# Output projection of a hybrid encoder layer: five pairs of row chunks as seven block products, from chunk 6 on

## The chip, the core and the metric

The kernel runs on one core of a Trainium2 chip: TensorE (PE, matmuls, with its weight loads as PEld), VectorE (DVE), ScalarE (ACT), GpSimd (POOL) and SyncE (SP), which issues the DMAs, almost all of them on one queue. The metric is the time of one execution in microseconds (us) on the device; what counts is the median of several runs. Profiles are of one execution each; their times are microseconds from the start of the span unless marked ns.

## What is computed

One layer of an encoder over 2048 rows of 1024 values. An input projection feeds two groups: gated linear attention (4 heads, columns 0 to 511 of the mixer's output) and latent attention (4 heads, columns 512 to 1023). What matters here is the end of it:

```python
def mla_branch(...):
    ...
    o = o.transpose(1, 0, 2, 3, 4).reshape(B, S, D_MLA)
    return o * jax.nn.silu(gate)

def hybrid_mixer(...):
    ...
    return jnp.concatenate([o_a, o_b], axis=-1) @ w_out

def reference(...):
    ...
        x = layer_norm(DEEPNORM_ALPHA * x + mixed, ln_g[layer], ln_b[layer])
```

`o_a` is the first group's output, `o_b` the second's; the output projection is a product of 2048x1024 by 1024x1024, followed by the residual and the layer norm of each row.

## The kernel before

All matmuls work on float32 numbers split in two parts, hi (rounded) and lo (the rest): a product is three matmuls, hi by hi, hi by lo and lo by hi (`mm3`, L454 to L456). hi is made by ScalarE (L400), lo by GpSimd or VectorE (L406).

The rows are 16 chunks of 128. Attention (from L1615) sweeps 16 blocks, each of one head and 512 query rows; in the last block's steps the output projection begins. Chunks 0 to 3 are multiplied between the last block's matmuls. Then come chunks 4 to 7 one by one, and then chunks 8 to 15 in four pairs.

A **single chunk** (`OutProj`) is 2 halves of 512 columns times 8 slices of the contraction times 3 matmuls, 48 matmuls of 512 columns. Its steps are: `load` (four DMAs: `of` from `oa_s` and `ob_s`, the gates `gr` from `gm_s` and the reciprocal sums from `r_s`), `hi` and `lo` of the first group, `gate` (GpSimd, two products), `hi` and `lo` of the second, the matmuls (`part`), `residual` (VectorE: alpha times x plus the product, read from PSUM, and the statistics of the half row), `finish_a` (mean, centring, and on ScalarE six small operations for the reciprocal root, here called the roots) and `finish_b` (scale and shift on VectorE, two stores of 256 KB).

A **pair** (`Pair`) multiplies two chunks, seen as a 2x2 block matrix (rows of the two chunks, columns of the two groups), by the 2x2 block weight in Strassen's manner: seven products P1 to P7 of 4x3 matmuls, 84 in place of 96. S1 to S4 are sums of the blocks (VectorE), A11, A12, A22 the blocks themselves. Products 5, 6, 7 and 4 take combined weights, which are prepared early, kept in DRAM and fetched by `fetch_t` ("1h" to "4l"; "4h" and "4l" are four DMAs each and overwrite half of the plain weights, so they wait for the last single chunk). Four PSUM banks, `pw0` to `pw3` (tags mb, x, o, ap), hold the products: P1 and P7 go to bank 0, P5 and P2 to bank 1, P6 to 2, P3 and P4 to 3. `copy` (L2065) copies P1 and later P7 from bank 0 on ScalarE; `sum` adds the copy to bank 2; `read` adds the banks to the rows of x.

**What sets the order.** From chunk 6 on every step has a place, a number on a time axis in us at which it would stand on TensorE; `put` collects them, they are sorted by place, and `in_order` ties the instructions of each engine, SyncE with its DMAs included, to that order. A place orders, it makes nothing wait by itself. Pair p begins at 4 x 5.44 + 19.05 p, and `PLACE_PAIR` holds the places of its steps relative to that. In the stretch before (chunks 2 to 5) `fixed` ties only ScalarE, GpSimd and SyncE to the order of the program; VectorE and TensorE are ordered by the planner that builds the program.

**Buffers.** Tiles of one tag share slots; the first write into a slot waits until all that read or write the tile before have ended, stores by DMA included. Those that matter here:

- tag "ofl" (one slot): `ol` (lo part of the last block's output), then `yc`, then the copies `pc` of the pairs;
- tag "ph" (three slots): the result rows `rr` of single chunks, and the x rows of each pair's second chunk;
- tag "xf" (two slots): `of` of the single chunks from 4 on and of the even-numbered pairs; odd-numbered pairs use the two SBUF rows of the layer norm's parameters, after `ln_psum` has copied these to PSUM;
- `gr[0]`, `gr[1]`: the gates of even and odd chunks.

The last attention block is closed late: `tot`, `oh`, `ol` (its output, split), `tsum` and `rcp` (sums and their reciprocals), `turn` and `y` (a transpose and the product with the value weights), and `rows` and `yc`, which copy the results on ScalarE and store them by DMA (L1801 and L1824). Before the change these last four have the places 5.40 (`turn`), 5.41 (`y`), 6.50 (`rows`) and 6.51 (`yc`), with chunk 6 beginning at 0.

Of the kernel before, what the change touches and what calls it, by code (L numbers as in the profile page):

```python
# [9 lines left out]
F32 = mybir.dt.float32  # L10
# [8 lines left out]
P = 128  # L19
# [3 lines left out]
NCH = S // P  # L23
# [68 lines left out]
    tot=11.2,  # L92
    half=11.7,
    fold=11.95,
    tsum=12.37,
    rcp=13.55,
    keep=14.21,
    turn=17.5,
    rows=17.55,
    oh=12.34,  # L100
    ol=12.99,
    y=16.55,
    yc=16.9,
# [27 lines left out]
)  # L131


PAIR0, PAIR_US = 8, 19.05
PLACE_PAIR = dict(
    load3=(-29.4, -31.5),
    load2=(-25.5, -31.5),
# [7 lines left out]
    last=dict(P1=0.0, P5=2.72, P6=5.44, P3=8.16, P2=10.88, P7=13.6, P4=16.32),  # L145
# [244 lines left out]
class K:  # L390
# [1224 lines left out]
    def attention(self):  # L1615
# [4 lines left out]
        with ExitStack() as ctx:  # L1620
# [6 lines left out]
            nb = len(blocks)  # L1627
# [140 lines left out]
            def tsum(i):  # L1768
                d = stt[i]
                d["x"] = close(i, [P, 4, P], f"sx{i}", (pA, "ap"))  # L1770
                for e in range(4 if i == nb - 1 else 2):
                    nc.tensor.transpose(d["x"][:, e], d["as"][:, 0, e * P:(e + 1) * P], self.ident)
# [68 lines left out]
            def put(place, fn, *a):  # L1841
                todo.append((place, len(todo), fn, a))
# [7 lines left out]
            for i in range(nb):  # L1850
                for j in range(NP):
                    t = NP * i + j
# [52 lines left out]
            rest = {c: o for c, o in enumerate(first)}  # L1905

            def load(c):
                if c < NCH:
                    rest[c] = dict(c=c)
                    op.load(rest[c])  # L1910

            def split(c):
                if c < NCH:
                    op.hi(rest[c], 0)
                    op.lo(rest[c], 0)
                    if c == PAIR0 - 1:
                        op.ln_psum(1)
                    op.gate(rest[c])
                    op.hi(rest[c], 1)
                    op.lo(rest[c], 1)  # L1920

            pairs = [Pair(op, p, PAIR0 + 2 * p + 1, PAIR0 + 2 * p) for p in range((NCH - PAIR0) // 2)]
            with fixed():
                load(4)
                for c in (2, 3):
                    op.load_res(rest[c])
                load(5)
                split(4)
                load(6)
                op.load_res(rest[4])  # L1930
                for c in (0, 1):
                    op.finish(rest[c])
                split(5)
                load(7)
                op.load_res(rest[5])
                op.fetch_t("2l")
                op.fetch_t("3h")
                for c in (2, 3):
                    op.residual(rest[c], 0)
                    op.residual(rest[c], 1)  # L1940
                    op.finish(rest[c])
            for c in (4, 5):
                with fixed():
                    if c == 4:
                        split(6)
                        pairs[0].load(1)
                        op.product(rest[4])
                    else:
                        op.load_res(rest[6])
                        tsum(nb - 1)  # L1950
                        with self.after(rest[4]["last"]):
                            rcp(nb - 1)
                        op.product(rest[5])
                        op.ln_psum(0)
                        pairs[1].load(0, "of")
                        op.fetch_t("3m")
                        split(7)
                        pairs[0].load(0)
                    op.finish(rest[c])
                if c == 4:  # L1960
                    with self.after(*last.values()), fixed():
                        for f in (tot, oh, ol):
                            f(nb - 1)

            todo.clear()
            half = 5.44
            put(4 * half - 0.01, op.pair_banks)
            for c in (6, 7):
                o, t = rest[c], 2 * half * (c - 6)
                if c == 7:  # L1970
                    put(-1, op.load_res, o)
                for n in range(2):
                    for k in range(NK):
                        put(t + half * n, op.part, o, k, (n,))
                    put(t + half * (2 if c % 2 else n + 1) + 0.05, op.residual, o, n)
                put(t + 2 * half + 1.3, op.finish_a, o)
                put(t + 2 * half + (5 if c == 6 else 4), op.finish_b, o)
            for place, f in ((5.4, turn), (5.41, y), (6.5, rows), (6.51, yc)):
                put(place, f, nb - 1)
            put(17.15, op.fetch_t, "4h")  # L1980
            put(17.16, op.fetch_t, "4l")
            op.last_pair = pairs[-1]
# [7 lines left out]
class Pair:  # L1990
# [131 lines left out]
    def put(self, put, T, last):  # L2122
        at = lambda place, fn, *a: put(T + place, fn, *a)
        P_, op = PLACE_PAIR, self.op
        first = P_[("first", "second")[self.p]] if self.p < 2 else {}
        if self.p:
            for r in (1, 0):
                at(P_[f"load{self.p}"][r], self.load, r, *(("gr",),) * (self.p == 1 and r == 0))
        for r in range(2):
            at(P_["res"][r], self.load_res, r)  # L2130
            for n in range(2):
                at(P_[f"gate{self.p}" if self.p < 3 else "gate"][r][n], self.gate, r, n)
        for n in self.OPERANDS:
            if n[0] == "S":
                at(first.get(f"a{n}", P_["add"][n]), self.add, n)
            at(first.get(f"h{n}", P_["hi"][n]), self.hi, n)
            at(first.get(f"l{n}", P_["lo"][n]), self.lo, n)
        bank = [lambda i=i: op.pw[i] for i in range(4)]
        t = P_["last" if last else "product"]
        b = dict(P1=0, P5=1, P6=2, P3=3, P7=1 if last else 0, P2=0 if last else 1, P4=3)  # L2140
        for n in t:
            if not (last and n == "P4"):
                at(t[n], self.product, n, bank[b[n]])
        e = P_["read_last" if last else "read"]
        at(e["c1"], self.copy, bank[0])
        at(e["U2"], self.sum, bank[2])
        if last:
            reads = (("R1", 0, 0, 0), ("R5", 1, 1, 1), ("R5b", 0, 1, 1), ("R2", 0, 1, 2), ("R3", 1, 1, 2), ("R4b", 1, 0, 2),
                     ("R6", 0, 1, 3), ("R7", 0, 0, b["P2"]), ("R3p", 1, 1, b["P7"]), ("R4p", 1, 0, b["P7"]))
        else:  # L2150
            at(e["c7"], self.copy, bank[b["P7"]])
            at(e["U3"], self.sum, bank[2])
            reads = (("R1", 0, 0, 0), ("R5", 1, 1, 1), ("R5b", 0, 1, 1), ("R2", 0, 1, 2), ("R6", 0, 1, 3), ("R3", 1, 1, 2),
                     ("R7", 0, 0, b["P2"]), ("R4", 1, 0, 3), ("R4b", 1, 0, 2))
        for n, r, h, x in reads:
            at(e[n], self.read, r, h, bank[x])
        if not last:
            at(e["bn22"], self.stats, 1, 1, 1)
            at(e["bn21"], self.stats, 1, 0, 0)
            at(e["sq"], self.squares, 0)  # L2160
            at(e["rs"], self.scale, 0)
            at(e["fa"][0], self.centre, 0)
            at(e["fa"][1], op.finish_a, self.rows[1])
            for r in range(2):
                if op.last_pair.p == self.p + 1:
                    at(e["late"][r], op.last_pair.finish_off, self.rows[r])
                else:
                    at(e["fb"][r], op.finish_b, self.rows[r])
            return
        at(P_["lnb"], self.copy_lnb)  # L2170
        at(e["bn12"], self.stats, 0, 1, 1)
        at(e["bn11"], self.stats, 0, 0, 0)
        at(e["bn22"], self.stats, 1, 1, 2, 3)
        for i, x in enumerate((3, 0)):
            cs, half = slice(256 * i, 256 * i + 256), lambda x=x: bank[x]()[:, :256]
            at(t["P4"] + PAIR_US / 14 * i, self.product, "P4", half, cs)
            at(t["P4"] + PAIR_US / 14 * (i + 1) + 0.45, self.read, 1, 0, half, cs)
            at(t["P4"] + PAIR_US / 14 * (i + 1) + 0.46, self.stats, 1, 0, i, 3, cs)
        at(e["fa"][0], op.finish_a, self.rows[0])
        at(e["fb"][0], self.finish_off, self.rows[0])  # L2180
        at(e["fa"][1], op.finish_a, self.rows[1])
        at(e["fb"][1], op.finish_b, self.rows[1])


class OutProj:
# [110 lines left out]
    def banks(self, o):  # L2296

        c = o["c"]
        if c == PAIR0 - 1:
            return [p.tile([P, 512], F32, tag=t, name=f"p{t}{c}") for p, t in self.single[2:]]  # L2300
        if c < 2 or c % 2:
            ps = self.ps.tile([P, 2, 512], F32, tag="pS", name=f"po{c}")
            return [ps[:, 0], ps[:, 1]]
        return [p.tile([P, 512], F32, tag=t, name=f"p{t}{c}") for p, t in self.single[:2]]
# [128 lines left out]
```

## Time and profile before

| | |
|---|---|
| median of 3 runs | 1276.6 us (1276.45 to 1277.14) |
| the profiled execution | 1275.83 us, its span 1274.0 us |
| mean granted TensorE clock | 0.998 of full |
| TensorE busy | 1253.9 us, 98% of the span |
| VectorE, ScalarE, GpSimd busy | 74%, 69%, 67% |
| first matmul of chunk 4, of chunk 6, of the first pair | 1145.14, 1167.36, 1189.95 |

A row of a timeline reads: start, duration, engine, line, operation, what it writes <- what it reads, size, count, and in brackets the idle time ahead of it with what ended it. "SPq" is SyncE issuing a DMA; its duration is that of the issue (waits included where rows are merged), not of the transfer. `pw` is any of the four banks of the pairs, told apart by the operands: `pw<-woh,A11h` is P1, `pw<-wt3h,S3h` is P7. A window's row gives, for a stretch, the busy time of the engines, the granted clock, the busy share of the 16 DMA engines and what they moved.

### The profile page before, as it was taken

The page shows a single profiled execution, that of the slowest core. Times are in us where ns is not written, and L with a number is a line of the kernel's source. Part 1 is how long each engine was busy: PE and PEld are TensorE (multiplying, and loading weights), DVE is VectorE, ACT ScalarE, POOL GpSimd, SP SyncE. Part 2 cuts the span into 40 slices and gives each one's busy share as a digit, 9 for nine tenths or more (in the row PEclk, how much of TensorE's full clock was granted, in tenths as well). Part 3 has the DMA queues.
Part 4 walks back from the last instruction along what each step waited for, and adds up shares of the span by engine and source line. Part 5 has one row for each costly group of instructions (what it writes and reads, how often), then busy time and mean ns, then how long its engine had stood idle before and what let it go on. Part 6 is the DMA issues. An engine that isn't in the chain of part 4 may idle for free.

```text
span 1274.0 us, 20184 instructions
## 1 busy us (share of the span) xinstructions
PE 1253.9 (98%) x6928; PEld 1109.6 (87%) x6928; DVE 938.3 (74%) x1702; ACT 875.2 (69%) x1553; POOL 849.4 (67%) x550
## 2 busy tenths in 40 slices
PE   7999999999999999999999999999999999999997
PEld 7999999999989999999788888888888888788886
DVE  6866675656675455555798888888888888738897
ACT  7765656766675655665688888888888888624365
POOL 0144545363667666672188888889999999965774
PEclk9999999999999999999999999999999999999999
DMA  9332524353575565565601111121223111568962
GB/s 300 96 96 63 168 81 156 106 155 102 191 254 169 180 222 184 182 196 166 177 1 42 42 42 42 42 58 59 59 58 91 53 43 31 174 207 297 342 214 98
DMA packets 122518, 166.81 MB, mean 131 GB/s; under 512 B 18502, under 2 KB 71118, under 8 KB 121776
## 3 DMA queue, kind: packets, MB, share of 16 engines
q1 hardware_dynamic: 114256, 163.39, 40.2%
q0 software_dynamic: 768, 2.10, 0.5%
q8 instruction: 55, 0.90, 0.4%
q10 hardware_dynamic: 7392, 0.03, 0.3%
q14 instruction: 47, 0.39, 0.2%
HBM read 106.72 MB, written 58.75 MB: 130 GB/s over the span
## 4 chain that ended last, share of the span: by engine, by line
PE 88%; ACT 3%; POOL 2%; DVE 2%; DMA 2%; issue 1%; SPq 1%; DVEq 0%; POOLq 0%; ACTq 0%
PE o L454 4%; PE o L456 4%; PE pS L1649 4%; PE o L455 4%; PE pS L1651 4%; PE pS L1650 4%; PE pS L1652 4%; PE pS L1653 4%; PE ipa L454 4%; PE ipa L456 4%; PE ipa L455 4%; PE pz L455 2%; PE pz L456 2%; PE pz L454 2%; PE ipg L454 2%; PE ipg L455 2%
## 5 line engine op out<-in xcount | busy, mean ns | idle before, releaser
L406 POOL TENSOR_TENSOR pl<-s,ph 128x1024 fp32r<-128x1024 f32 x128 | 306.1, 2414 | 56.4 <-ACT ph L400 56.4
L1671 DVE TENSOR_TENSOR rm<-pS,rm 128x512 f32<-128x512 f32 x210 | 144.7, 689 | 26.3 <-ACT s L1658 20.7
L1695 DVE TENSOR_TENSOR s<-s,mb 128x1024 f32<-128x1024 f32 x128 | 151.1, 1212 | 9.4 <-PE mb L1689 9.3
L1658 ACT ACTIVATE s<-pS 128x1024 f32<-128x1024 f32 x128 | 131.2, 1025 | 37.6 <-PE pS L1653 33.2
L400 ACT ACTIVATE ph<-s 128x1024 fp32r<-128x1024 f32 x128 | 134.9, 1057 | 13.4 <-PE o L456 12.7
L1699 ACT ACTIVATE s<-s 128x1024 f32<-128x1024 f32 x128 | 131.4, 1051 | 13.4 <-DVE s L1695 13.3
L454 PE MATMUL ipa<-wah,xah 128*128 128x384 f32 (+1 forms) x384 | 130.2, 339 | 6.3 <-ACT wah L400 6.2
L1112 POOL TENSOR_TENSOR Us<-Us,cw 128x512 f32<-128x512 f32 x16 | 18.2, 1134 | 175.8 <-DVE Us L1110 167.7
L455 PE MATMUL ipa<-wal,xah 128*128 128x384 f32 (+1 forms) x384 | 125.2, 326 | 0.1
L456 PE MATMUL ipa<-wah,xal 128*128 128x384 f32 (+1 forms) x384 | 125.2, 326 | 0.0
L1649 PE MATMUL pS<-qh,ckvT_h 128*128 128x512 f32 x256 | 102.5, 401 | 0.8 <-DVE rm L1671 0.4
L454 PE MATMUL o<-ph,vh 128*128 128x512 f32 x256 | 101.1, 395 | 0.0
L1652 PE MATMUL pS<-rh,krs 128*128 128x512 f32 x256 | 99.8, 390 | 0.0
L1650 PE MATMUL pS<-ql,ckvT_h 128*128 128x512 f32 x256 | 99.8, 390 | 0.0
L456 PE MATMUL o<-ph,vl 128*128 128x512 f32 x256 | 99.8, 390 | 0.0
L1651 PE MATMUL pS<-qh,ckvT_l 128*128 128x512 f32 x256 | 99.8, 390 | 0.0
L1653 PE MATMUL pS<-rl,krs 128*128 128x512 f32 x256 | 99.8, 390 | 0.0
L455 PE MATMUL o<-pl,vh 128*128 128x512 f32 x256 | 99.8, 390 | 0.0
L1722 DVE TENSOR_TENSOR ap<-ap,s 128x512 f32<-128x512 f32 x120 | 83.1, 693 | 3.5 <-ACT ap L1714 0.7
L454 PEld LDWEIGHTS ipa<-wah,xah 128*128 128x128 f32 x384 | 73.4, 191 | 7.3 <-ACT wah L400 6.7
L454 PE MATMUL pz<-xch,wzh 128*128 128x256 f32 x256 | 74.8, 292 | 0.0
L455 PEld LDWEIGHTS ipa<-wal,xah 128*128 128x128 f32 x384 | 73.4, 191 | 1.3 <-DVE wal L406 0.7
(446 smaller groups left out, 3895.9 us busy)
## 6 DMA issues: line engine op xcount, KB each, us to landing
xcf<-xT_dram SPq DMA_DIRECT2D x16, 512.0 KB, 4.9
xr<-x_dram SPq DMA_DIRECT2D x16, 512.0 KB, 6.9
xaf<-xT_dram SPq DMA_DIRECT2D x14, 512.0 KB, 3.8
wb<-wO_dram SPq DMA_DIRECT2D x16, 256.0 KB, 3.0
oib<-oi_s SPq DMA_DIRECT2D x16, 256.0 KB, 3.8
qdb<-qd_s SPq DMA_DIRECT2D x16, 256.0 KB, 4.3
SU<-su_s SPq DMA_DIRECT2D x16, 256.0 KB, 4.6
ub<-u_s SPq DMA_DIRECT2D x16, 256.0 KB, 4.2
```

Of the source, the lines that this page charges most:

```text
L400: return nc.scalar.activation(dst, src, AF.Copy).ins
L406: return e.tensor_tensor(dst, src, hi.bitcast(F32), ALU.subtract).ins
L454: mm(out, ah, bh, start=start, stop=False)
L455: mm(out, ah, bl, start=False, stop=False)
L456: mm(out, al, bh, start=False, stop=stop)
L1649: mm(ps[:, e], kh, qh, start=True, stop=False)
L1650: mm(ps[:, e], kh, ql, start=False, stop=False)
L1651: mm(ps[:, e], kl, qh, start=False, stop=False)
L1652: mm(ps[:, e], kr, rh, start=False, stop=False)
L1653: mm(ps[:, e], kr, rl, start=False, stop=True)
L1671: V.tensor_tensor(d["rm"], src[:, e], d["rm"], ALU.max)
L1695: V.tensor_tensor(s, s, d["mb"][:, None, :].to_broadcast([P, 2, QB]), ALU.subtract)
```

## The change

The pairs begin with chunk 6 in place of chunk 8 (`PAIR0` 6), so that chunks 6 to 15 are five pairs, the first of chunks 7 and 6; only chunks 4 and 5 are multiplied singly, and they are now the ones ordered by place, with their first matmul at place 0. Of the pairs from the fourth on, the loads use the places `load3`.

In the fixed stretch `split` is cut in two halves (hi, lo and gate; second hi and lo). The `finish` of chunk 0 stands ahead of chunk 4's first half, that of chunk 1 between its halves, and that of chunk 2 between the halves of chunk 5; with them move their stores, on SyncE ahead of the loads that follow. `tot`, `oh` and `ol` of the last block come between chunk 4 and chunk 5. The loads of chunks 6 and 7 are those of the first pair.

In the part ordered by place, with chunk 4 at 0 and chunk 5 at 10.88: `ln_psum(0)` at 1.5, the second half of the second pair's loads at 6.4, `tsum` 10.87, `rcp` 10.90, `fetch_t("3m")` 11.9, `fetch_t("4h")` and `("4l")` at 17.15 and 17.16 as before, `turn` 21.70, `y` 21.71, `rows` 22.00, `yc` 22.01. Chunk 5 takes the banks mb and x, as chunk 4 does, and no longer the PSUM tiles "pS".

```diff
-PAIR0, PAIR_US = 8, 19.05
+PAIR0, PAIR_US = 6, 19.05
...
-            def split(c):
-                if c < NCH:
+            def split(c, j):
+                if j == 0:
                     op.hi(rest[c], 0)
                     op.lo(rest[c], 0)
                     if c == PAIR0 - 1:
                         op.ln_psum(1)
                     op.gate(rest[c])
+                else:
                     op.hi(rest[c], 1)
                     op.lo(rest[c], 1)
...
                 load(5)
-                split(4)
-                load(6)
+                op.finish(rest[0])
+                split(4, 0)
+                op.finish(rest[1])
+                split(4, 1)
+                op.residual(rest[2], 0)
+                op.residual(rest[2], 1)
+                pairs[0].load(1)
                 op.load_res(rest[4])
-                for c in (0, 1):
-                    op.finish(rest[c])
-                split(5)
-                load(7)
+                with self.after(*last.values()):
+                    for f in (tot, oh, ol):
+                        f(nb - 1)
+                split(5, 0)
+                op.finish(rest[2])
+                split(5, 1)
+                pairs[0].load(0)
                 op.load_res(rest[5])
                 op.fetch_t("2l")
                 op.fetch_t("3h")
-                for c in (2, 3):
-                    op.residual(rest[c], 0)
-                    op.residual(rest[c], 1)
-                    op.finish(rest[c])
-            for c in (4, 5):
...
+                op.residual(rest[3], 0)
+                op.residual(rest[3], 1)
+                op.finish(rest[3])
...
-            for c in (6, 7):
-                o, t = rest[c], 2 * half * (c - 6)
-                if c == 7:
-                    put(-1, op.load_res, o)
+            for c in (4, 5):
+                o, t = rest[c], 2 * half * (c - 4)
...
-                    put(t + half * (2 if c % 2 else n + 1) + 0.05, op.residual, o, n)
+                    put(t + half * (n + 1) + 0.05, op.residual, o, n)
...
-            for place, f in ((5.4, turn), (5.41, y), (6.5, rows), (6.51, yc)):
+            for place, f in ((10.87, tsum), (10.9, rcp), (21.7, turn), (21.71, y), (22.0, rows), (22.01, yc)):
                 put(place, f, nb - 1)
+            put(1.5, op.ln_psum, 0)
+            put(6.4, pairs[1].load, 0, "of")
+            put(11.9, op.fetch_t, "3m")
             put(17.15, op.fetch_t, "4h")
             put(17.16, op.fetch_t, "4l")
...
-                at(P_[f"load{self.p}"][r], self.load, r, *(("gr",),) * (self.p == 1 and r == 0))
+                at(P_[f"load{min(self.p, 3)}"][r], self.load, r, *(("gr",),) * (self.p == 1 and r == 0))
...
-        if c == PAIR0 - 1:
-            return [p.tile([P, 512], F32, tag=t, name=f"p{t}{c}") for p, t in self.single[2:]]
-        if c < 2 or c % 2:
+        if c < 2 or c == PAIR0 - 3:
```

More of the change, by code (lines that the diff above doesn't have):

```diff
@@ L1907, in load @@
             def load(c):
-                if c < NCH:
-                    rest[c] = dict(c=c)
-                    op.load(rest[c])
-            def split(c):
-                if c < NCH:
+                rest[c] = dict(c=c)
+                op.load(rest[c])
+            def split(c, j):
+                if j == 0:
                     op.hi(rest[c], 0)
@@ L1937, in attention @@
                 op.fetch_t("3h")
-                for c in (2, 3):
-                    op.residual(rest[c], 0)
-                    op.residual(rest[c], 1)
-                    op.finish(rest[c])
-            for c in (4, 5):
[L1943 to L1963, printed above, removed]
+                op.residual(rest[3], 0)
+                op.residual(rest[3], 1)
+                op.finish(rest[3])
             todo.clear()
@@ L1974, in attention @@
                         put(t + half * n, op.part, o, k, (n,))
[L1975 removed]
+                    put(t + half * (n + 1) + 0.05, op.residual, o, n)
                 put(t + 2 * half + 1.3, op.finish_a, o)
[L1977 to L1978 removed]
+                put(t + 2 * half + (5 if c == 4 else 4), op.finish_b, o)
+            for place, f in ((10.87, tsum), (10.9, rcp), (21.7, turn), (21.71, y), (22.0, rows), (22.01, yc)):
                 put(place, f, nb - 1)
+            put(1.5, op.ln_psum, 0)
+            put(6.4, pairs[1].load, 0, "of")
+            put(11.9, op.fetch_t, "3m")
             put(17.15, op.fetch_t, "4h")
```

## The prediction

> **What bounds the kernel now.** I read the page first (busy shares, then the chain that ended last), then TensorE's timeline from the end of attention on, then the same stretch of ScalarE and of SyncE's DMA queue, and last the windows.
>
> ```profile
> span 1274.0 us, 20184 instructions
> PE 1253.9 (98%) x6928; PEld 1109.6 (87%) x6928; DVE 938.3 (74%) x1702; ACT 875.2 (69%) x1553; POOL 849.4 (67%) x550
> ...
> PE 88%; ACT 3%; POOL 2%; DVE 2%; DMA 2%; issue 1%; SPq 1%; DVEq 0%; POOLq 0%; ACTq 0%
> ```
>
> The chain is 88% matmuls: whatever is taken off TensorE without making it wait comes off the end. This is TensorE around the change (start, us, engine, line, operation):
>
> ```profile
> 1145.14 0.39 PE L454 MATMUL pmb<-woh,oh 128*128 128x512 f32 x1
> ...
> 1167.36 0.39 PE L454 MATMUL pmb<-woh,oh 128*128 128x512 f32 x1
> ...
> 1172.80 0.27 PE L1794 MATMUL rt<-ident,rc 128*4 128x128 f32 x1
> ...
> 1173.61 0.39 PE L454 MATMUL px<-woh,oh 128*128 128x512 f32 x1
> ...
> 1189.95 0.39 PE L454 MATMUL pw<-woh,A11h 128*128 128x512 f32 x1
> ...
> 1200.83 0.39 PE L454 MATMUL pw<-wt3h,S3h 128*128 128x512 f32 x1
> ...
> 1208.99 0.39 PE L454 MATMUL pw<-woh,A11h 128*128 128x512 f32 x1
> ```
>
> The rows are the starts of chunk 4, chunk 6, the last block's `rt` and `y` (0.81 us, 1172.80 to 1173.61), the first pair's P1, its P7, and the second pair's P1. A pair is 1208.99 - 1189.95 = 19.04 us; P7 comes 1200.83 - 1189.95 = 10.88 us after P1. From here T is a first pair's P1; in this run T is 1189.95. The DMA engines, by contrast, are full in just this stretch (busy time of the engines, granted clock, DMA share, GB/s):
>
> ```profile
> 1174.00:1184.00 10.00, 10.00 (x45) 8.26 (x45) 7.13 (x14) 3.38 (x12) 5.43 (x5) 1.00 0.98 327
> 1184.00:1194.00 10.00, 10.00 (x45) 8.28 (x45) 8.00 (x13) 3.57 (x10) 8.61 (x7) 1.00 1.06 368
> 1194.00:1204.00 10.00, 10.00 (x45) 8.26 (x44) 8.50 (x15) 4.18 (x11) 7.29 (x7) 1.00 1.01 343
> 1204.00:1214.00 10.00, 10.00 (x46) 8.28 (x45) 8.06 (x14) 5.96 (x12) 8.63 (x8) 1.00 0.99 322
> ```
>
> Some 340 GB/s (the mean of the four) is what the queue carries there, with a share of 1: what is issued later lands later.
>
> **The change part by part.** *Products.* From chunk 4's start to T stand now four chunks plus 0.81 us, 44.81 us. Two chunks with the four transposes of `tsum` are 1167.36 - 1145.14 = 22.22 us, so the new T is 1145.14 + 22.22 + 0.81 = 1168.17. What follows is five pairs in place of four. The gain on TensorE is 44.81 - 23.03 - 19.04 = **2.74 us**, and no more: 84 matmuls in place of 96.
>
> *A wait at P7.* The copy `pc` of P1 (place T + 2.78, ScalarE) is written into the slot "ofl", which has one buffer. `yc`, the last block's value rows, uses the same slot. So `pc` cannot be written before the store of `yc` has landed. That a writer waits for a store of the tile before it is seen elsewhere in this kernel: `qal` takes the slot of `gm`, and VectorE waits for the store of `gm`.
>
> ```profile
> DVE qal L406 <- DMA gm_s<-gm: 2.7, 1, 2.7
> ```
>
> At present this costs nothing, as `yc` has place 6.51 and `pc` comes long after:
>
> ```profile
> 1177.95 0.57 ACT L1823 ACTIVATE yc<-y 128x512 f32<-128x512 f32 x1
> ...
> 1198.04 0.58 ACT L2065 ACTIVATE pc<-pw 128x512 f32<-128x512 f32 x1
> ```
>
> ```profile
> 1187.08 0.34 SPq L1824 DMA_DIRECT2D ob_s<-yc  x1
> ...
> 1193.52 3.75 SPq L2241 DMA_DIRECT2D woh<-wt4h_s  x4
> 1197.33 3.02 SPq L2241 DMA_DIRECT2D wol<-wt4l_s  x4
> 1200.75 1.23 SPq L2364 DMA_DIRECT2D out_dram<-rr  x2
> ```
>
> The change moves `rows` and `yc` to 22.00 and 22.01. ScalarE still makes `yc` at about T, but SyncE issues in the order of places, and at 17.11 to 17.16 stand the gates of chunk 9 and the eight pieces of the fourth combined weight, 2 MB. The store of `yc`, issued ahead of these weights now, falls behind them. P7 is written into bank 0, which `pc` must have read: the PE queue stops at P7, and P2, P4 and all later pairs stand behind it. Behind `pc` on ScalarE wait the next pair's hi parts (S1, S2, S3); U2 on VectorE waits for `pc` too.
>
> When does that store land? First way: the DMA right behind those weights was issued at 1200.75, T + 10.8, and such a store takes 6.7 us to land here, so T + 17.5.
>
> ```profile
> out_dram<-rr SPq DMA_DIRECT2D x16, 256.0 KB, 6.7
> ```
>
> ```profile
> DMA to landing us min/median/max: 2.3/3.3/4.3
> ```
>
> Lowest bound: the 3.3 us that stores of `yc` took over the whole span (second row), T + 14.1. Second way: from the loads of chunk 7 to `yc` I count in the new order 41 pieces of 256 KB (of 7 four, x rows of 5 two, weights 2l and 3h eight, out 3 two, of 8 four, of 9 two, x of 7 and 6 four, 3m two, out 4 two, gates 9 two, weights four eight, `yc` one), 10.7 MB, 31.6 us at 340 GB/s. The loads of chunk 7 wait for the lo part that frees their buffer:
>
> ```profile
> 1145.02 0.19 ACT L2352 ACTIVATE ln_l<-u 128x1 f32<-128x1 f32 x1
> ...
> 1148.11 0.62 ACT L400 ACTIVATE oh<-of 128x512 fp32r<-128x512 f32 x1
> ```
>
> ```profile
> 1155.59 0.33 SPq L2272 DMA_DIRECT2D of<-oa_s  x1
> ```
>
> The two chains of roots (1145.02 to 1148.11) leave the place ahead of chunk 5's split, and the last block's `ofh` and the copy of ln_b come into it, so I take 2 us off 1155.59 and some 2.5 us for the two stores ahead in the queue: transfers run from 1156. That ends at 1187.6, T + 19.4. Upper bound: 322 GB/s, the slowest row, from 1157.5: 1190.9, T + 22.7. I take the middle of the two ways, T + 18.5, both being readings of the full queue. With the copy's 0.58 us and 0.1 us of hand-over, P7 starts at T + 19.2 and not at T + 10.88: **8.3 us late**, between 3.9 (T + 14.1) and 12.5 (T + 22.7).
>
> *A smaller wait at P1.* Chunk 5 now uses the banks mb and x, the first two of the pair; residual 5 must read mb before P1. Its rr slot (three buffers, the pair's x rows taking one in between) is that of chunk 3, freed when out 3 lands. Out 3 stands behind 2l and 3h, as now:
>
> ```profile
> 1158.97 0.38 SPq L2255 DMA_DIRECT2D wt3h<-wt3h_s  x1
> 1159.44 5.91 SPq L2364 DMA_DIRECT2D out_dram<-rr  x4
> ```
>
> Of the 41 pieces, 16 come up to out 3: 12.3 us from 1156, 1168.3; with 0.7 us of VectorE P1 would start near 1169.1, 0.9 us late (0 to 3). It costs nothing at the end as long as P7's date is set by a landing; without that wait it is lost whole. The same holds for chunk 5's first matmul, which needs residual 4 and its x rows.
>
> *The clock after the wait.* At the kernel's opening 288-column matmuls follow each other at 0.24 us and then at 0.13 us:
>
> ```profile
> 7.34 0.44 PE L454 MATMUL ipa<-wah,xah 128*128 128x288 f32 x1
> 7.58 0.44 PE L455 MATMUL ipa<-wal,xah 128*128 128x288 f32 x1
> ...
> 12.18 0.40 PE L456 MATMUL ipa<-wah,xal 128*128 128x288 f32 x1
> ...
> 12.55 0.29 PE L455 MATMUL ipa<-wal,xah 128*128 128x288 f32 x1
> 12.68 0.29 PE L456 MATMUL ipa<-wah,xal 128*128 128x288 f32 x1
> ```
>
> ```profile
> 1266.00:1268.00 2.00, 0.42 (x4) 0.22 (x2) 1.79 (x7) 0.03 (x1) 1.77 (x2) 1.00 0.30 114
> 1268.00:1270.00 2.00, 0.00 (x0) 0.00 (x0) 1.59 (x3) 1.46 (x6) 0.00 (x0) 0.62 0.40 149
> ```
>
> At the end the granted clock falls to 0.62 some two us after the last matmul. So idling for 8 us makes the next matmuls slow. The opening has some 20 slow ones that lose about 0.12 us each: 2.4 us, which I take as the nearest row (0 if the clock holds, 3.0 for the whole 6 us at half rate). The Trainium skill, "TensorE: Matmul & The Clock Gate", section "What's actually happening", has the clock halved after an idle window of about 3.4 us and restored after as much busy time; half of 3.4 us would be 1.7 us, and the sum 0.7 us lower. No row here can say which window applies.
>
> *The rest, at nothing.* The roots and stores of chunks 0 and 1 go ahead of the loads of chunk 6, whose buffer is freed by chunk 4's last lo part as now; cover gone, it is a later load of 6, which the pair needs only at T. `tot`, `oh`, `ol` and both copies of the layer-norm rows move to idle ScalarE and VectorE. The added pair puts on VectorE what a pair has now, 16.70 us in 19:
>
> ```profile
> 1209.00:1228.00 19.00, 19.00 (x85) 15.76 (x84) 16.70 (x26) 11.09 (x30) 14.90 (x12) 1.00 0.80 258
> ```
>
> *Sum:* -2.74 + 8.3 + 2.4 = +8.0 us. The profiled execution took 1275.83 us, so 1283.8; on the median of the runs, 1276.6, it is **1284.6 us**.
>
> **Rivals.** (a) *No wait at P7*: the store of `yc` lands by T + 10.2, in time for copy and hand-over, and residual 5 is not late; then only the products count: 1276.6 - 2.7 = 1273.9. For it: TensorE stands still nowhere in this stretch now, and a store of `yc` alone lands in 3.3 us. Against it: the 2 MB ahead, which were issued from T + 3.6 on. (b) *Only the wait at P1* decides: -2.7 + 0.9 is 1274.8, with 0 to 3 us a time within 0.2% of the median. Against it the same order of places. (c) *The standstill spreads*: ScalarE is some 16 us behind (T + 2.78 to T + 18.5), and the second pair's S operands come late as well. P7, P2 and P4 give them 8.2 us, U2, R2, the add, three hi parts and the lo parts need about as much; if they miss by 4 us, 1288.6. Against it: P1 of that pair needs A11 alone, whose hi part precedes the copy.
>
> **How the numbers follow.** Forecast 0.77, (a) 0.08, (b) 0.07, (c) 0.08. A run can tell 0.2%, 2.55 us. The forecast's own bounds are -2.7 + 3.9 = +1.2 and -2.7 + 12.5 + 2.4 = +12.2, thus 1277.8 to 1288.8; the low end needs every bound at once, the high end is widened by (c): 1278.5 to 1290.0. Faster 0.08 (a), same 0.07 (b), slower 0.85.
>
> **What would show it.** In the changed trace: idle of TensorE ahead of `pw<-wt3h,S3h` of the first pair, ended by ScalarE's `pc`, that one by the landing of `ob_s<-yc`, issued after the last `wol<-wt4l_s`; matmuls at half pace behind it; P1 of the first pair near 1168 to 1170. I am wrong if `pc` starts soon after P1 with no idle, if P7 runs at T + 10.9, or if TensorE stops elsewhere.

## The result, and the profile after

The changed kernel takes 1286.09 us (median of 6 runs, 1284.28 to 1288.16); the kernel before took 1276.53 us in the same session (6 runs, 1276.11 to 1277.14). The ratio is 1.0076, with a 95% interval of 1.0065 to 1.0086. The change is 9.6 us slower. Its runs also scatter over 3.9 us, those of before over 1.0 us (in the later sessions over 2.5 to 4.0 us, two far slower executions left out). The profiled execution took 1284.28 us, the quickest of the six; its span is 8.5 us longer than that of before.

From the page of the changed kernel: the span, the busy times, and the shares of the chain that ended last by engine.

```profile
span 1282.5 us, 20183 instructions
PE 1252.9 (98%) x6916; PEld 1107.7 (86%) x6916; DVE 940.1 (73%) x1708; ACT 882.0 (69%) x1567; POOL 853.2 (67%) x553
...
PE 84%; DVE 4%; DMA 4%; ACT 3%; POOL 2%; issue 2%; SPq 1%; DVEq 0%; POOLq 0%; ACTq 0%
```

There are 12 matmuls fewer, as there should be. PE's part of the chain fell from 88% to 84%, and DMA, VectorE and issue have what it lost. Next, what TensorE waited for from 1085 us on (us in total, times, longest); before the change only the third of these rows was there.

```profile
PE pw L454 <- ACT pc L2051: 6.7, 1, 6.7
PE pmb L454 <- DVE rr L2314: 2.1, 1, 2.1
PE y L454 <- DVE rc L1781: 0.3, 1, 0.3
```

Two new waits, once each. The rows of TensorE's timeline that belong to them are the first matmul of chunk 5, the first of the first pair's P1, three of its P7, the first of its P2, and the second pair's P1.

```profile
1158.92 0.47 PE L454 MATMUL pmb<-woh,oh 128*128 128x512 f32 x1 [2.07 <-DVE rr L2314]
...
1170.95 0.47 PE L454 MATMUL pw<-woh,A11h 128*128 128x512 f32 x1
...
1188.77 0.80 PE L454 MATMUL pw<-wt3h,S3h 128*128 128x512 f32 x1 [6.68 <-ACT pc L2051]
...
1190.21 0.63 PE L454 MATMUL pw<-wt3h,S3h 128*128 128x512 f32 x1
...
1191.49 0.46 PE L454 MATMUL pw<-wt3h,S3h 128*128 128x512 f32 x1
...
1192.96 0.39 PE L454 MATMUL pw<-woh,A12h 128*128 128x512 f32 x1
...
1198.41 0.39 PE L454 MATMUL pw<-woh,A11h 128*128 128x512 f32 x1
```

P7 should come at 1170.95 + 10.88 = 1181.83 and comes at 1188.77: 6.9 us late. ScalarE and SyncE's queue show why.

```profile
1170.93 0.60 ACT L1823 ACTIVATE yc<-y 128x512 f32<-128x512 f32 x1 [0.43 <-PE y L456]
...
1188.12 0.60 ACT L2051 ACTIVATE pc<-pw 128x512 f32<-128x512 f32 x1 [11.43 <-DMA ob_s<-yc]
```

```profile
1174.91 4.45 SPq L2227 DMA_DIRECT2D woh<-wt4h_s  x4
1179.67 2.69 SPq L2227 DMA_DIRECT2D wol<-wt4l_s  x4
1182.76 0.27 SPq L1801 DMA_DIRECT2D r_s<-rt  x1
1183.45 0.34 SPq L1824 DMA_DIRECT2D ob_s<-yc  x1
```

`yc` is made at 1170.93, but its store is issued at 1183.45, behind the eight pieces of the fourth combined weight. ScalarE stands idle for 11.43 us until the store has landed, then writes `pc` into the slot that `yc` had, and P7 follows. The windows over the standstill (busy time of PE, PEld, DVE, ACT and POOL with counts, then granted clock, DMA share, GB/s) show the queue full and the clock going down.

```profile
1182.00:1184.00 2.00, 0.09 (x1) 0.00 (x0) 1.84 (x3) 0.00 (x0) 0.00 (x0) 1.00 1.05 385
1184.00:1186.00 2.00, 0.00 (x0) 0.00 (x0) 0.14 (x1) 0.00 (x0) 0.00 (x0) 0.70 1.05 391
1186.00:1188.00 2.00, 0.00 (x0) 0.00 (x0) 0.00 (x0) 0.00 (x0) 0.00 (x0) 0.50 1.00 374
1188.00:1190.00 2.00, 1.23 (x3) 1.05 (x4) 1.22 (x2) 1.12 (x2) 0.69 (x1) 0.50 0.77 242
```

P7 takes 1192.96 - 1188.77 = 4.19 us instead of 2.72, so the clock costs 1.5 us. The other pairs take 19.04 us each, as before. The sum against the profile of before: chunk 4 begins 0.2 us later, the wait at chunk 5 costs 2.1 and its surroundings some 0.4, P7 is 6.9 late, the clock 1.5, the products give back 2.7: +8.4, where the span grew by 8.5.

The wait at chunk 5 comes from VectorE's order. In its timeline the finish of chunk 3 (here its centring, L2330) stands ahead of residual 4, which must empty the bank that chunk 5 is written into.

```profile
1155.76 2.41 DVE L2330 SCALAR_TENSOR_TENSOR rr<-rr,mv,lng 128x512 f32<-128x512 f32 x2
1158.10 0.68 DVE L2314 SCALAR_TENSOR_TENSOR rr<-xr,pmb 128x512 f32<-128x512 f32 x1
```

### The profile page after: what moved, and what is told of

Same layout as the page of the kernel before. It is cut to its first block, busy times and chain, and to the rows that moved or that the text cites. A ratio compares the mean times of both kernels' runs of the same rounds, so it can differ in the third digit from the quotient of the medians.

```text
span 1282.5 us, 20183 instructions
## 1 busy us (share of the span) xinstructions
PE 1252.9 (98%) x6916; PEld 1107.7 (86%) x6916; DVE 940.1 (73%) x1708; ACT 882.0 (69%) x1567; POOL 853.2 (67%) x553
## 4 chain that ended last, share of the span: by engine, by line
PE 84%; DVE 4%; DMA 4%; ACT 3%; POOL 2%; issue 2%; SPq 1%; DVEq 0%; POOLq 0%; ACTq 0%
PE pS L1649 4%; PE pS L1651 4%; PE pS L1650 4%; PE pS L1652 4%; PE pS L1653 4%; PE o L454 4%; PE o L455 4%; PE o L456 4%; PE ipa L454 4%; PE ipa L456 4%; PE ipa L455 4%; PE pw L454 2%; PE pw L456 2%; PE pw L455 2%; PE pz L455 2%
```

## The experiments

Each edit is against the changed kernel unless said otherwise. Ratios are to the kernel before in the same session, where its medians were 1275.9 to 1276.8 us. The theory at the start: P7's date is the landing of the store of `yc`; whatever else is late in front of it is absorbed. The rivals: the earlier roots cost the time, or the volume on the queue does, whatever shares a slot with what.

**The wait itself.** `pc` goes into the slot of `ofh`, so that it shares nothing with `yc`.

```diff
-        self.cp = self.op.bp.tile([P, QB], F32, tag="ofl", name=f"pc{self.p}", bufs=1)
+        self.cp = self.op.bp.tile([P, QB], F32, tag="ofh", name=f"pc{self.p}", bufs=1)
```

> The copies of P1 and P7 go into the slot of ofh (free once y is computed) instead of that of yc; nothing else is changed. Theory (the copy waits for the landing of the store of yc): the idle of TensorE ahead of the first P7 (6.7 us in the changed kernel's profile) and its slow clock behind it (about 1.5 us) go away, the copy starts within some 4 us of the end of P1, and the time is 1286.1 - 8.2 = 1277.9 us (1277 to 1279.5). Rival 1 (the full DMA queue itself is the bound): the fourth combined weight, which landed at about 1187, now stops P4, due at T + 16.3 = 1187.3; idle there of 1 to 3 us, 1279 to 1281. Rival 2 (ScalarE is held by something else): 1286, as before.

1278.63 us (10 runs, 1276.93 to 1279.51), ratio to before 1.0013 (1.0004 to 1.0022): some 7.5 us of the 9.6 come back with one word. P7 runs at 1183.37, 10.9 us after P1, and P4 does not wait for the fourth combined weight, as the first rival had it. What remains are two waits of TensorE, and behind the first of them a low clock:

```profile
PE pmb L454 <- DVE rr L2314: 2.2, 1, 2.2
PE pw L454 <- ACT pc L2051: 1.2, 1, 1.2
```

```profile
1160.00:1162.00 2.00, 2.00 (x6) 1.54 (x5) 1.97 (x5) 0.00 (x0) 0.64 (x1) 0.50 0.86 269
1162.00:1164.00 2.00, 2.00 (x8) 1.61 (x8) 1.93 (x4) 0.43 (x1) 0.00 (x0) 0.77 1.07 443
```

**The place of the store.** The slot stays shared, but the store of `yc` is issued ahead of the fourth combined weight.

```diff
-            put(17.15, op.fetch_t, "4h")
-            put(17.16, op.fetch_t, "4l")
+            put(22.05, op.fetch_t, "4h")
+            put(22.06, op.fetch_t, "4l")
```

> The fourth combined weight is fetched behind the stores of rows and yc (places 22.05 and 22.06 for 17.15 and 17.16); the slot stays shared. Theory: the store of yc leaves some 8 us earlier, lands near 1183, and P7, due at 1181.8, starts near 1184; the idle shrinks from 6.7 to about 2 us and is too short for the clock to fall, the weights land 0.7 us later and still in time for P4: 1286.1 - 4.7 - 1.5 = 1279.9 us (1278.5 to 1281.5). Rival (the order on the queue does not matter, the sharing alone does, or the idle comes from the amount of DMA work): 1285 to 1287.

1279.56 us (7 runs, 1277.94 to 1282.88), ratio 1.0025 (1.0012 to 1.0037). The store is issued 5.4 us sooner:

```profile
1178.08 0.34 SPq L1824 DMA_DIRECT2D ob_s<-yc  x1
```

ScalarE's timeline still shows the landing of the store as what ends the idle time, but at 1183.68, and P7 follows at 1184.34 after 1.03 us:

```profile
1183.68 0.60 ACT L2051 ACTIVATE pc<-pw 128x512 f32<-128x512 f32 x1 [6.51 <-DMA ob_s<-yc]
```

Slot and place are both needed for the damage; taking away either takes most of it away (by the ratios, 1.0076 becomes 1.0013 or 1.0025).

**Work into the standstill.** The first pair's P3 is multiplied three times over, which puts 2 x 2.72 = 5.4 us of matmuls ahead of P7 (each repeat starts its sum anew).

```diff
-                at(t[n], self.product, n, bank[b[n]])
+                for _ in range(3 if self.p == 0 and n == "P3" else 1):
+                    at(t[n], self.product, n, bank[b[n]])
```

> The first pair's P3 is multiplied three times into the same bank (the same result each time), 24 matmuls or 5.4 us more work on TensorE right ahead of P7; nothing else is changed. Theory (P7's date is a landing): the 5.4 us fit into the idle of 6.7 us and cost nothing, about 1.3 us of idle is left, and as TensorE has stood still only briefly P7 runs at full clock: 1286.1 - 1.5 = 1284.6 us (1283.5 to 1286.5). If only the landing holds and the clock falls anyway: 1286. Rival (TensorE's own work sets the end): 1291.5.

1285.8 us (4 runs, 1284.0 to 1287.67), ratio 1.0077 (1.006 to 1.0093): 5.4 us of added matmuls cost nothing. `pc` still waits for the landing:

```profile
1189.20 0.60 ACT L2051 ACTIVATE pc<-pw 128x512 f32<-128x512 f32 x1 [11.16 <-DMA ob_s<-yc]
```

P7 follows at 1189.85, and its matmuls are at full pace (its first row and that of P2; 2.85 us in all):

```profile
1189.85 0.50 PE L454 MATMUL pw<-wt3h,S3h 128*128 128x512 f32 x1
...
1192.70 0.39 PE L454 MATMUL pw<-woh,A12h 128*128 128x512 f32 x1
```

The 1.3 us of idle that were expected ahead of P7 are not there: P1 came only at 1173.38, 2.4 us later than in the changed kernel, so TensorE's own work reaches to 1173.38 + 10.88 + 5.44 = 1189.70. The clock's 1.5 us do not show in the time, as `pc` started 1.1 us later than in the changed kernel.

**The roots alone.** In the kernel before, `finish` of chunks 0 and 1 is put ahead of the split of chunk 4, and nothing else is changed.

```diff
                 load(5)
+                for c in (0, 1):
+                    op.finish(rest[c])
                 split(4)
                 load(6)
                 op.load_res(rest[4])
-                for c in (0, 1):
-                    op.finish(rest[c])
```

> The kernel before, with one part of the change alone: the finish of chunks 0 and 1 (roots, scaling, stores) stands ahead of the split of chunk 4 and so ahead of the loads of chunk 6. Theory: TensorE has no wait there, so the time stays that of the kernel before, 1276.5 us within 0.7. Rival (the earlier stores put the loads behind and hold TensorE, a share of the loss of the changed kernel): 1278 to 1279.

1277.3 us (10 runs), beside 1276.79 for before, ratio 1.0005 (0.9996 to 1.0015). The earlier roots of these two chunks cost nothing that can be told from no change; the interval leaves room for up to 1.9 us.

**What lies in front, with the slot shared.** Residual 4's first half goes ahead of the finish of chunk 3, so that chunk 5 need not wait for it; the x rows of chunk 6 are loaded after residual 5, so that residual 5 gets the slot that chunk 2 has left and need not wait for out 3 to land.

```diff
                 op.residual(rest[3], 1)
-                op.finish(rest[3])
...
-                    put(t + half * (n + 1) + 0.05, op.residual, o, n)
+                    put(t + half * (n + 1) + (0.05 if c + n > 4 else -0.64), op.residual, o, n)
...
+            put(4.85, op.finish_a, rest[3])
+            put(4.88, op.finish_b, rest[3])
...
-            at(P_["res"][r], self.load_res, r)
+            at(P_["res"][r] if (self.p, r) != (0, 1) else -5.38, self.load_res, r)
```

> The change as it is, pc still in the slot of yc, with the same two edits (residual 4's first half ahead of the roots of chunk 3, x rows of chunk 6 after residual 5). Theory: P7's date is set by the landing of the store of yc, which stands behind the same transfers; P1 comes some 2.5 us earlier, P7 waits that much longer, and the time stays: 1286.1, between 1284.8 and 1287.5. Rival, the waits add up: 1286.1 - 2.5 = 1283.6 or, with the half clock at chunk 5, 1282.

1287.05 us (4 runs), ratio 1.0092 (1.0079 to 1.0106). The wait at chunk 5 is gone, P1 comes 1.6 us sooner (1169.31 instead of 1170.95), and the time is no lower: P7's wait has grown from 6.7 to 9.5 us.

```profile
PE pw L454 <- ACT pc L2052: 9.5, 1, 9.5
```

**The same with `pc` in its own slot.** Now P7 does not hide them, and they should count.

> The change with a slot of its own for pc, and besides: residual 4's first half goes ahead of the roots of chunk 3 on VectorE (so chunk 5 need not wait for it), and the x rows of chunk 6 are loaded after residual 5 instead of before it (so residual 5's rr takes the slot that chunk 2 has left and need not wait for the landing of out 3). Theory: the two waits of the own-slot run (2.2 us at chunk 5 with some 1.7 us of half clock behind it, and P1 at 1172.46 where 1168.4 would be without waits) are lost whole once P7 does not wait, so about 4.1 us come back: 1274.5, between 1273.5 and 1276. Rival: the DMA queue is the limit, and the fourth combined weight lands only near 1187, where P4 (P1 + 16.3 us = 1184.7) needs it: then 1276.9, and the trace shows P4 waiting for a DMA.

1278.45 us (10 runs), ratio 1.0019 (1.001 to 1.0028): no quicker than with the slot alone. Both expectations fail. The first pair's P1 comes at 1168.15, 4.3 us sooner than with the slot alone, as meant, but the pairs are longer. These are the P1 of the five pairs:

```profile
1168.15 0.39 PE L454 MATMUL pw<-woh,A11h 128*128 128x512 f32 x1
...
1188.22 0.39 PE L454 MATMUL pw<-woh,A11h 128*128 128x512 f32 x1
...
1209.21 0.50 PE L454 MATMUL pw<-woh,A11h 128*128 128x512 f32 x1 [1.13 <-ACT pc L2052]
...
1229.84 0.50 PE L454 MATMUL pw<-woh,A11h 128*128 128x512 f32 x1 [1.14 <-ACT pc L2052]
...
1249.92 0.50 PE L454 MATMUL pw<-woh,A11h 128*128 128x512 f32 x1 [0.65 <-ACT pc L2052]
```

They take 20.07, 20.99, 20.63 and 20.08 us instead of 19.04; 5.6 us are lost. VectorE waited for x rows five times in this stretch:

```profile
DVE xr L2062 <- DMA xr<-x_dram: 10.7, 5, 2.9
```

A new theory follows: the x rows stand on the queue behind outputs which VectorE must finish first, so a delay of VectorE comes back to it one pair later.

**Only residual 4 moved**, `pc` in its own slot.

> The change with a slot of its own for pc and only residual 4's first half ahead of the roots of chunk 3. Theory: the wait at chunk 5 is gone (under 0.4 us), but residual 5 still needs the landing of out 3 near 1170, so P1 comes near 1171.7 and not near 1168.4: 1277.9, between 1277.0 and 1279. Rival, the wait at chunk 5 is the only one that counts: 1275.

1278.41 us (10 runs), ratio 1.0018 (1.0009 to 1.0028). The wait at chunk 5 is gone, and the first pair waits 2.9 us for residual 5 in its place, followed by some 6 us at a granted clock of 0.50 (1171 to 1177).

**Less ahead of the weight.** As the run with both waits taken away, with the output of chunk 4 and the load of chunk 9's gates sent behind it.

```diff
-                put(t + 2 * half + (5 if c == 4 else 4), op.finish_b, o)
+                put(t + 2 * half + (6.42 if c == 4 else 4), op.finish_b, o)
...
-    load1=(-23.7, -35.9),
+    load1=(-23.6, -35.9),
```

> As the run with both waits taken away, and besides the output of chunk 4 (512 KB) and the gates of chunk 9 (512 KB) are sent behind the fourth combined weight's first pieces or among them, so that the weight lands up to 3 us earlier. If P4 waited for the weight in that run, this one is faster by that wait, 1274 to 1275; if it did not, the two are the same within 0.7 us.

1277.62 us (11 runs), ratio 1.0015 (1.0006 to 1.0024): within the scatter of the run with both waits taken away (1278.45). P4's wait of 0.3 us is gone, and the pairs still take 19.06, 21.06, 20.96 and 20.92 us. P4 was not what counted.

**The x rows early**, with the own slot, residual 4's move, less ahead of the weight, and a slot reserved early for residual 5.

```diff
-            at(P_["res"][r], self.load_res, r)
+            at(((-16.86, -9.74), (-23.4, -23.39))[self.p][r] if self.p < 2 else -25.4 + 0.01 * r, self.load_res, r)
```

> The change with the slot of its own for pc, residual 4's first half ahead of the roots of chunk 3, residual 5 free of out 3, chunk 4's output sent behind the gates, and now the x rows of every pair loaded ahead of the outputs of the pair before the last instead of behind them. Theory: with all waits at the front taken away, pairs take 20 to 21 us instead of 19.04, since VectorE waits 1.5 to 2.9 us in each for x rows, which stand on the queue behind outputs that VectorE has to finish first: a ring that hands its delay on. With the rows early the ring is cut, the pairs take 19.0 to 19.4 us, and the products' 2.74 us appear: 1273.9, between 1273 and 1275.5. Rival: VectorE and ScalarE have no room in a pair and the ring closes by another way (the copies of P7, the lo parts), pairs stay above 20 us: 1277.5.

1280.45 us (7 runs), ratio 1.003 (1.0019 to 1.0041), slower. Two of the edits work against each other: the x rows of chunk 8 take the slot of chunk 4's result, whose output this version sends late, and SyncE stood until it had landed, with everything behind it.

```profile
SPq L2012 <- DMA out_dram<-rr: 4.6, 1, 4.6
```

Residual 5 waited for an output as well (4.42 us), though its slot was reserved ahead; why it got that slot was not followed up. So this run says nothing on the theory.

**The x rows early, and the own slot, nothing else** (the same line with -8.0 for chunk 6 and -23.635 and -23.63 for the second pair).

> The change with only the slot of its own for pc and the x rows early; the waits at chunk 5 (2.2 us, with half clock behind it) and at residual 5 stay. Theory: first P1 near 1172 to 1172.5 as in the own-slot run, pairs of 19.0 to 19.4: 2 us below the own-slot run, 1276.5, between 1275.5 and 1277.5. Rival: the x rows were not what made the pairs longer, then 1278.6 as in the own-slot run.

VectorE's waits for x rows between 1140 and 1275 us, with the slot alone and then with the rows early too:

```profile
DVE xr L2061 <- DMA xr<-x_dram: 6.7, 4, 2.2
```

```profile
DVE xr L2061 <- DMA xr<-x_dram: 2.1, 1, 2.1
```

In this execution P1 comes at 1171.53 and all four pairs that follow it take 19.04 to 19.06 us, so with the rows early nothing in them is late. But the time is 1277.73 us (11 runs, 1275.19 to 1278.93), just outside what was expected, with a ratio of 1.0013 (1.0004 to 1.0022), the same as with the slot alone. The profile here is of the second quickest of 11 executions (1276.45 us), that of the slot alone of the slowest of 10 (1279.51 us). So the rows early take VectorE's waits away, and a gain in time is not shown.

**Out 3 ahead of the weights 2l and 3h**, with own slot, residual 4 and early x rows.

```diff
-                op.fetch_t("2l")
-                op.fetch_t("3h")
...
+            put(4.885, op.fetch_t, "2l")
+            put(4.89, op.fetch_t, "3h")
```

> The early x rows with the slot of its own for pc, residual 4's first half ahead of the roots of chunk 3, and the combined weights 2l and 3h (2 MB) sent behind out 3 instead of ahead of it, x rows of chunk 6 ahead of the rest of the third combined weight. Theory: out 3 lands near 1165 instead of near 1170, so residual 5 no longer waits for it, P1 starts at 1168.2 to 1168.5 without any stop before it, the pairs take 19.04 each as in the run with early rows alone, and the last matmul ends 2.2 to 2.6 us sooner than before: 1274.2, between 1273.5 and 1275.5. Rival: with P1 3 us sooner the weights of the fourth block land too late for P4 (they landed 5.3 us before P1 of the second pair in the run with early rows alone, which leaves P4 about 2 us short): one stop of up to 2 us, 1276.

1279.22 us (11 runs), ratio 1.0022 (1.0013 to 1.0031), above both expectations. P1 starts at 1168.67 without any stop, and then other things are late, at P3 (a lo part, GpSimd), at P4 (the weight) and at a copy:

```profile
PE pw L456 <- POOL S4l L406: 2.0, 1, 2.0
PE pw L454 <- ACT pc L2052: 1.8, 1, 1.8
PE pw L455 <- DMA wol<-wt4l_s: 0.6, 1, 0.6
```

**Both waits and the x rows**, 2l and 3h where they were; x rows of chunk 7 at -15.37, those of chunk 6 at -5.38, the output of chunk 4 behind them.

> The run with both waits at the front taken away (slot of its own for pc, residual 4's first half ahead of the roots of chunk 3, x rows of chunk 6 after residual 5), and the x rows of the later pairs early as in the run with early rows alone; x rows of chunk 7 a place sooner, output of chunk 4 behind the x rows of chunk 6. Weights 2l and 3h stay ahead of out 3. Theory, the ring of x rows made the pairs longer: first P1 at 1168.2, second near 1188 (x rows of chunk 6 land near 1180 and hold VectorE for 2 us), then pairs of 19.04: the last matmul ends near 1264.6 and the time is 1274.8, between 1274 and 1276.3. Rival, from the run with every front taken away: it is the volume on the queue up to the end of the fourth combined weight, whatever its order; what the first P1 gains is lost in the second and third pair, which take over 20 us each, and the time is 1277.5 to 1278.5.

1277.23 us (11 runs, 1274.94 to 1279.54), ratio 1.0005 (0.9995 to 1.0014): between the two expectations, the lowest ratio of the versions with five pairs, and not to be told from the kernel before. The first P1 comes at 1169.26; the pairs take 19.74, 21.40, 19.24 and 19.04 us. The third pair's P1 waits:

```profile
1210.40 0.50 PE L454 MATMUL pw<-woh,A11h 128*128 128x512 f32 x1 [2.19 <-ACT pc L2052]
```

In GpSimd's timeline it can be followed back to a load of the third pair: a gate waits for it (`ob_s`, the second group's half) for 4.04 us, and the gates that follow come late and beside VectorE's sums. Two of these sums are the sources of S2 and S3, whose hi parts stand ahead of the copy of P7 on ScalarE.

```profile
1197.13 1.30 POOL L2015 TENSOR_TENSOR of<-of,gr 128x512 f32<-128x512 f32 x1 [4.04 <-DMA of<-ob_s]
...
1203.39 3.44 POOL L2015 TENSOR_TENSOR of<-of,gr 128x512 f32<-128x512 f32 x2
```

The runs of the versions whose `pc` has its own slot in one table, beside before and changed, from the timelines of TensorE (us). Each row is one execution, whose time is in the second column:

| run | this execution | first P1 | from P1 to P1 of the pairs | last matmul ends |
|---|---|---|---|---|
| before | 1275.83 | 1189.95 | 19.04, 19.04, 19.04 | 1266.4 |
| changed | 1284.28 | 1170.95 | 27.46, 19.04, 19.04, 19.04 | 1274.9 |
| own slot | 1279.51 | 1172.46 | 19.07, 19.04, 20.87, 19.27 | 1270.1 |
| both waits gone | 1278.89 | 1168.15 | 20.07, 20.99, 20.63, 20.08 | 1269.5 |
| only residual 4 moved | 1279.62 | 1171.29 | 21.97, 19.04, 19.04, 19.33 | 1270.2 |
| less ahead of the weight | 1278.92 | 1167.95 | 19.06, 21.06, 20.96, 20.92 | 1269.5 |
| x rows early, with the earlier edits | 1281.37 | 1171.35 | 19.17, 22.29, 20.80, 19.04 | 1272.0 |
| x rows early, own slot | 1276.45 | 1171.53 | 19.06, 19.04, 19.04, 19.04 | 1267.1 |
| out 3 first | 1280.56 | 1168.67 | 22.30, 21.05, 20.78, 19.04 | 1271.2 |
| both waits, x rows | 1277.44 | 1169.26 | 19.74, 21.40, 19.24, 19.04 | 1268.0 |

Wherever P1 comes before 1170, 3 us or more go again in the pairs, at waits that differ from run to run. None of these runs left bytes out, so that the volume on the queue is the limit is the reading that fits, not a thing shown.

## Why the prediction was right, point by point

- *Products, -2.74*: as predicted, 12 matmuls less and pairs of 19.04 us. But no version with five pairs came out ahead of before; whatever else was mended, the gain was spent on waits.
- *The wait at P7*: the mechanism is the predicted one, shown by the slot (1278.63 without it), by the place of the store (1279.56) and by added work that is free (1285.8). The date was 1187.4 (1168.17 + 19.2) and was measured at 1188.77. Of the two ways to the landing, the count of pieces came close: T + 19.4 (T is 1168.17), where `pc` starts at 1188.12, T + 19.95. The other had the issue at T + 10.8 and the landing 6.7 us later; the store was issued at 1183.45, T + 15.3, and `pc` starts 4.7 us after that, so two errors partly cancel in it. The term was 8.3 and is 6.9, seen from P1, since P1 itself came at 1170.95 and not at 1168.17.
- *The wait at P1*: predicted to start near 1169.1, 0.9 us late, and to be absorbed. The delay was 2.8 us, most of it from chunk 5's first matmul, which the prediction named and costed at nothing. Its cause was seen only in part: not the x rows, but VectorE's order, the finish of chunk 3 ahead of residual 4. That it is absorbed was right: taking it away left 1287.05. It is no longer nothing where P7 does not wait.
- *The clock, 2.4*: 1.5 us. The nearest row, the kernel's opening, was too dear. The Trainium skill, "TensorE: Matmul & The Clock Gate", section "What's actually happening", gives full clock back after some 3.4 us of busy time; the estimate from that page, half of it or 1.7 us, would have been the better size. In the trace the pace is full again sooner, 2.7 us after P7's start (from 1188.77 to 1191.49).
- *The rest, at nothing*: holds for the roots of chunks 0 and 1 (1.0005, 0.9996 to 1.0015). The finish of chunk 3 ahead of residual 4 had no term, and it is what chunk 5 waited for.
- *Rivals*: (a) and (b) put the time without P7's wait at 1273.9 and 1274.8. With the wait taken away it is 1278.63. In that run's profile P1 comes 4.3 us after 1168.17, with the wait at chunk 5 and the low clock behind it, and the later pairs lose 2.1 us more; (b) had 0.9 us for the first and nothing for the second. Why the later pairs lose time is argued, not shown: their loads come on the same queue and have 22 us less to land than before the change, and in the changed kernel P7's standstill gave that time back. (c) did not happen: after 1198.41 all pairs take 19.04 us.

The sum, +8.0, is 0.5 us off in the profiled execution (+8.5). That it is so near is partly luck: P7's date was put 1.4 us too early and the clock's term 0.9 us too high, and the two errors cancel in part. On the medians it is 1.5 us off (1284.6 against 1286.09); the profile is of the quickest of the six runs, and what makes single runs differ was not measured.

## What to carry to other kernels

When a store is moved behind large loads on a queue that is issued in order, look up what reuses the slot it is stored from: the next writer waits for the landing, not for the engine that read the tile. A single long wait hides shorter ones before and after it; what the change is worth without that wait isn't the sum without its term, as shown by the 1278.6 that were measured where 1273.9 was worked out. A part that is started earlier also needs its data earlier: count the bytes that have to land by then before counting the work saved (advice that fits these runs; none of them tests it alone).

## What was not expected of the hardware

*Short idle, low clock.* An idle of 2.2 us ahead of chunk 5 brought the granted clock to 0.50 in the run with the own slot, and chunk 5 took 1.7 us longer than it should (windows above). The clock does not fall at once. The first three matmuls behind the wait start some 0.3 us apart, then they start 0.43 us apart for some 3.4 us, and then 0.23 us apart:

```profile
1159.66 0.63 PE L456 MATMUL pmb<-woh,ol 128*128 128x512 f32 x1
1160.08 0.63 PE L454 MATMUL pmb<-woh,oh 128*128 128x512 f32 x1
...
1163.01 0.39 PE L455 MATMUL pmb<-wol,oh 128*128 128x512 f32 x1
1163.24 0.39 PE L456 MATMUL pmb<-woh,ol 128*128 128x512 f32 x1
```

The same is seen behind chunk 5's wait in the runs with the store first, with the added work and with the x rows early alone (idle of 1.90, 2.35 and 1.84 us, then some 3.4 us at half pace). In the changed kernel nearly the same idle, 2.07 us, left the clock at 1.00:

```profile
1158.00:1160.00 2.00, 1.08 (x5) 0.93 (x6) 2.00 (x4) 1.00 (x2) 0.92 (x1) 1.00 0.62 138
1160.00:1162.00 2.00, 2.00 (x11) 1.63 (x10) 1.97 (x5) 0.00 (x0) 0.38 (x1) 1.00 0.95 358
```

So one wait may cost its own length or nearly twice that. The Trainium skill, "TensorE: Matmul & The Clock Gate", section "What's actually happening", has the window run free of the kernel, which would make the cost a matter of phase. That these runs differ by phase was not shown, and all these idles are shorter than the 3.4 us that the page gives for its idle window. This may be a part of the scatter of all versions that stop at chunk 5.

*VectorE and GpSimd side by side.* In the run with the own slot a sum of the blocks on VectorE takes 0.68 us at 1162.86, in a window (1162 to 1164, above) in which GpSimd is not busy at all:

```profile
1162.86 0.68 DVE L2026 TENSOR_TENSOR s<-of 128x512 f32<-128x512 f32 x1
```

In the last run another such sum takes 1.67 us beside the two gates of GpSimd at 1203.39, which take 3.44 us there; a single gate takes 1.30 (1197.13).

```profile
1204.01 1.67 DVE L2027 TENSOR_TENSOR of<-of,of 128x512 f32<-128x512 f32 x1
```

The Trainium skill, "SBUF — State Buffer", section "SBUF: two separate sides", has the two engines take turns on a port pair when VectorE reads two inputs from SBUF. The rows agree in that both are slowed; late gates thus cost twice, once by themselves and once on VectorE. It also reaches the operation that chunk 5 waits behind: the centring of chunk 3 takes 2.41 us in the changed kernel (1155.76, above) beside two gates that run from 1154.48 to 1157.63, and the same operation takes 1.40 us in the kernel before, where GpSimd is idle:

```profile
1160.64 1.40 DVE L2346 SCALAR_TENSOR_TENSOR rr<-rr,mv,lng 128x512 f32<-128x512 f32 x2
```

How long chunk 5 would have waited without these gates was not run.
